# Attention on one core: scores three steps ahead, next to the product with V and the transpositions

## The chip, the cores and the metric

The kernel runs on one core of a Trainium2 chip. The metric is the device time of one launch in microseconds (us); of several runs the median is taken. Five engines work side by side, each through its own list of instructions in order, and wait for one another by semaphores: TensorE (PE in the profile; its weight loads are PEld), VectorE (DVE), ScalarE (ACT), GpSimd (POOL), and SyncE (SP), which only starts transfers between the main memory and the core's own memory SBUF. TensorE writes its results to a small memory of its own, PSUM, which VectorE and ScalarE read.

## What is computed

Two layers over 2048 positions of width 1024. The first is a gated MLP, which the change does not touch. The second is an attention in which each chunk of 64 positions sees its own chunk and the eight before it; this is the part that matters here:

```python
def one_chunk(args):
    c, qc = args
    kc = lax.dynamic_slice_in_dim(k_pad, c * CHUNK, B_BAND, axis=1)
    vc = lax.dynamic_slice_in_dim(v_pad, c * CHUNK, B_BAND, axis=1)
    sc = jnp.einsum('bqhd,bkhd->bhqk', qc, kc).astype(jnp.float32) + bias
    sc = jnp.where(valid[None, None, None, :], sc, NEG_INF)
    p = jax.nn.softmax(sc, axis=-1).astype(vc.dtype)
    return jnp.einsum('bhqk,bkhd->bqhd', p, vc)
...
return (o * jax.nn.silu(z)) @ w_out
```

There are 16 heads of 64 channels. Q, K and the gate z are projections of the normalised stream.

## The kernel before

**Tiling.** The positions are cut into four tiles `t` of 512, the heads into eight pairs `p`. For one tile and one pair there are eight steps `u`: head `u // 4` of the pair, block `u % 4` of 128 queries. The band of such a block is at most 640 keys. In tile 0 there are no keys ahead of the tile, so the four blocks have 128, 256, 384 and 512 keys; from tile 1 on all have 640.

**One step.** `score` (line 1383) multiplies Q and K (line 1398; each operand is split into a high and a low part, so two or four matmuls), into the PSUM tile `s`, of which there is one buffer. VectorE adds the bias and takes the row's extreme (line 1406, tiles `pr` and `nm`), ScalarE takes the exponential and its sum (line 1413), VectorE the reciprocal of the sum (line 1416), GpSimd scales the row (line 1417). `flip` (line 1422) transposes the row in blocks of 128 keys on TensorE (line 1433) into the PSUM tile `tp`, of which there is also one buffer; ScalarE copies it as the high part (line 1437), VectorE subtracts it for the low part (line 1438); both go to the tile `pt`, one buffer for a head. `value` (line 1443) multiplies a head's transposed rows and V (line 1458, result `pv`), once in four steps. `pr`, `nm` and `sl` have four buffers each.

**The filler.** Beside these steps TensorE has matmuls that none of them waits for at once: the projections of the *next* pair (tile `pj`; `project` makes Q first, then K, `gate` makes z; 8 pieces each), and the output product of the tile before (`bo`, split by a Strassen scheme into pieces). A piece is three matmuls of 512 columns (lines 111 to 113: high by high, high by low, low by high). A generator `ahead` yields after each piece; `take(gen, n)` draws `n` pieces. After the K projection ScalarE and VectorE write its high and low part (lines 1335 and 1336); the scores of the next pair need them.

**What sets the order.** The loop at lines 1893 to 1934 lists the work of a step. With `total` pieces in a pair (24 in tile 0 and for the first four pairs of tile 1; 30 to 38 where output pieces are added; 25 at the very last pair), the count drawn by the middle and by the end of step `u` is

```python
upto = total * (2 * u + 1) // per
...
upto = total * (2 * u + 2) // per
```

and `per` is 16, so the pieces are spread over all eight steps; at the last pair of tiles 0 to 2 it is 11. A step lists: the score of step `u + 2`, the first half of its pieces, the product with V (at `u` 4 for the pair's first head, at `u` 0 for the last head of the pair before), the transposition of step `u`, the postponed work of VectorE and ScalarE, the second half of its pieces. Scores of the next pair begin at `u` 6. A scheduler then walks through the listed work when the program is built, and moves an instruction forward where the ones listed ahead of it are not ready by its own reckoning; so the order on each engine is near the listed one and not equal to it. On the chip that order is fixed.

## Time and profile before

| | |
|---|---|
| time, median of 3 runs (lowest, highest) | 2655.66 us (2654.55, 2656.12) |
| span of the profiled execution, from its first to its last instruction | 2652.0 us |
| of it ahead of the attention's first scores | about 1560 us |
| mean granted TensorE clock over the span | 0.996 |

The profile is of one execution; it gives that execution's span and no time of its own by the clock that the runs are timed with. The median of the runs is 3.7 us above the span. A row of the profile that groups instructions names the source line, the engine, the operation, the output and the input, then the count, the busy time, the mean length of one, and the idle time of the engine just before them with what ended it. Matmuls overlap in their pipeline: a matmul of 512 columns is shown 0.39 us long, and the next begins 0.23 us after it. So the rate of TensorE is read from the starts.

### The profile page before, as it was taken

The numbers are of one execution on the slowest core, as the hardware profiler recorded it, in microseconds if no ns is written. First come the engines' busy times: TensorE is split into PE (matmuls) and PEld (weight loads), VectorE is DVE, ScalarE is ACT, GpSimd is POOL, SyncE is SP. The second block draws the span as 40 slices with busy tenths as digits, with TensorE's granted clock in tenths as the row PEclk, the third lists the DMA queues.
The fourth block names the chain that finished last, engine by engine and source line by source line (L and its number), as shares of the span: only waits on it lengthen the run. The fifth ranks groups of instructions, "written<-read, shape, count | busy, mean of one in ns | idle before, by whom it ended". The sixth has DMA issues, their size and how long they took to land. (4 is left out here: it accounts for less than half of the span.)

```text
span 2652.0 us, 37980 instructions
## 1 busy us (share of the span) xinstructions
PE 2608.0 (98%) x12960; PEld 2181.4 (82%) x12960; DVE 1885.1 (71%) x2944; ACT 1303.2 (49%) x2303; POOL 897.2 (34%) x874
## 2 busy tenths in 40 slices
PE   8999999999999999999989999999999999999997
PEld 7888888888888888888878878888888888888886
DVE  5655676865767667757767767777778777877677
ACT  5422243442533434343356456666666655666564
POOL 3611334142152322203234434344332232332245
PEclk9999999999999999999999999999999999999999
DMA  7898998989989869967776597778787666875667
GB/s 286 313 344 329 346 370 323 323 323 338 330 302 313 308 233 324 331 206 270 280 251 214 186 280 229 231 245 263 252 270 254 226 204 224 255 230 161 195 224 251
DMA packets 273856, 718.72 MB, mean 271 GB/s; under 512 B 28800, under 2 KB 68736, under 8 KB 273664
## 3 DMA queue, kind: packets, MB, share of 16 engines
q1 hardware_dynamic: 273664, 716.31, 78.4%
q8 instruction: 103, 1.69, 0.3%
q14 instruction: 89, 0.73, 0.1%
HBM read 531.12 MB, written 174.59 MB: 266 GB/s over the span
## 5 line engine op out<-in xcount | busy, mean ns | idle before, releaser
L111 PE MATMUL P<-T,S 128*128 128x512 f32 x1248 | 496.2, 398 | 2.1 <-ACT S L434 2.1
L112 PE MATMUL P<-T,S 128*128 128x512 f32 x1248 | 488.2, 391 | 1.1 <-DVE T L437 1.1
L113 PE MATMUL P<-T,S 128*128 128x512 f32 x1248 | 488.6, 391 | 0.0
L1417 POOL TENSOR_SCALAR pr<-pr,sl 128x640 f32<-128x640 f32 (+4 forms) x256 | 209.7, 819 | 530.4 <-DVE sl L1416 445.2
L111 PE MATMUL pj<-hh_b,wh_b 128*128 128x512 f32 x768 | 320.4, 417 | 0.0
L113 PE MATMUL pj<-hh_b,wl_b 128*128 128x512 f32 x768 | 305.0, 397 | 1.2 <-DVE wl_b L229 1.1
L112 PE MATMUL pj<-hl_b,wh_b 128*128 128x512 f32 x768 | 303.4, 395 | 0.1
L1413 ACT ACTIVATE pr<-pr,nm 128x640 f32<-128x640 f32 (+4 forms) x256 | 195.5, 764 | 188.1 <-DVE nm L1406 186.6
L113 PEld LDWEIGHTS P<-T,S 128*128 128x128 f32 x1248 | 234.9, 188 | 50.5
L111 PEld LDWEIGHTS P<-T,S 128*128 128x128 f32 x1248 | 235.5, 189 | 46.9 <-ACT S L434 2.3
L112 PEld LDWEIGHTS P<-T,S 128*128 128x128 f32 x1248 | 235.6, 189 | 46.1 <-DVE T L437 1.3
L1438 DVE TENSOR_TENSOR pt<-tp,pt 128x640 fp32r<-128x640 f32 (+4 forms) x256 | 188.4, 736 | 43.7 <-ACT pt L1437 41.1
L1406 DVE CUSTOM_DVE_ANT_0 pr<-s,bias 128x640 f32<-128x640 f32 (+4 forms) x256 | 187.9, 734 | 35.7 <-PE s L1398 29.8
L1437 ACT CAST pt<-tp 128x640 fp32r<-128x640 f32 (+4 forms) x256 | 159.0, 621 | 54.0 <-PE tp L1433 49.8
L1433 PE MATMUL tp<-ident,pr 128*128 128x128 f32 x1120 | 166.7, 275 | 8.6 <-DVE pt L1438 7.3
L113 PEld LDWEIGHTS pj<-hh_b,wl_b 128*128 128x128 f32 x768 | 144.7, 188 | 36.4 <-DVE wl_b L229 3.8
L1433 PEld LDWEIGHTS tp<-ident,pr 128*128 128x128 f32 x1120 | 130.7, 140 | 43.3 <-issue 13.7
L111 PEld LDWEIGHTS pj<-hh_b,wh_b 128*128 128x128 f32 x768 | 145.8, 190 | 18.1 <-ACT wh_b L228 1.6
L1458 PEld LDWEIGHTS pv<-pt,V 128*128 128x128 f32 x896 | 143.3, 189 | 20.8 <-DVE pt L1438 3.9
L112 PEld LDWEIGHTS pj<-hl_b,wh_b 128*128 128x128 f32 x768 | 145.8, 190 | 17.1 <-DVE hl_b L186 0.6
L1458 PE MATMUL pv<-pt,V 128*128 128x256 f32 (+3 forms) x896 | 154.5, 320 | 2.2 <-ACT pt L1437 1.1
L229 DVE TENSOR_TENSOR wl_b<-raw_b,wh_b 128x1024 fp32r<-128x1024 f32 x96 | 120.4, 1255 | 28.5 <-ACT wh_b L228 27.8
(294 smaller groups left out, 5725.9 us busy)
## 6 DMA issues: line engine op xcount, KB each, us to landing
S<-hsd SPq DMA_DIRECT2D x288, 512.0 KB, 5.3
rw<-in_w_a SPq DMA_DIRECT2D x108, 512.0 KB, 6.3
A<-ytd SPq DMA_DIRECT2D x72, 512.0 KB, 5.7
raw_b<-wk SPq DMA_DIRECT2D x72, 512.0 KB, 4.3
hsd<-S SPq DMA_DIRECT2D x56, 512.0 KB, 4.9
V<-vhd SPq DMA_DIRECT2D x56, 512.0 KB, 5.4
bias<-reld SPq DMA_DIRECT2D x64, 320.0 KB, 4.2
va<-vd SPq DMA_DIRECT2D x32, 512.0 KB, 5.5
```

The source lines that it names most:

```text
L111: first = mm(ps, lh, rh, start=first, stop=False)
L112: mm(ps, lh, rl, start=False, stop=False)
L113: mm(ps, ll, rh, start=False, stop=last)
L229: tv(wl[:], raw[:], wh[:].bitcast(F32), op=sub)
L1406: nc.vector.tensor_tensor_reduce(out=pr[:, c0:].rearrange("p (a b) -> p a b", a=nseg), in0=ps[:, :nseg, :w], in1=bias[:, c0:].rearrange("p ...
L1413: nc.scalar.activation(pr[:, c0:], pr[:, c0:], AF.Exp, scale=-1.0, bias=nm[:], accum_out=sl[:])
L1417: nc.gpsimd.tensor_scalar(pr[:, c0:], pr[:, c0:], sl[:], 1.0, op0=ALU.mult, op1=ALU.mult)
L1433: ins = tpose(tp[:, b, :], pr[:, b * P : (b + 1) * P], ident[:])
L1437: nc.scalar.copy(oh, tp[:, b0:5, :].rearrange("p a b -> p (a b)"))
L1438: nc.vector.tensor_tensor(pt[:, 2560 + o + b0 * P : 2560 + o + 640], tp[:, b0:5, :].rearrange("p a b -> p (a b)"), oh.bitcast(F32), op=ALU ...
L1458: mm(po[:, q0 * P : q1 * P], vtl[t, p][:, i, hs], rhs, start=(i == blocks[0] and j == 0), stop=(i == 7 and j == 1),)
```

## The change

Three things are changed in the listing of the work; nothing in what is computed, and no tile or buffer count.

1. `score` now lists the score matmuls and the line 1406 alone, and gives back a function `weigh` that lists the exponential, the reciprocal and the scaling. It is called behind `flip`.
2. The scores run three steps ahead (`AHEAD = 3`), so those of the next pair begin at `u` 5. The score, the product with V and the transposition of a step are listed one behind the other; all pieces of the step come behind them.
3. `per` is 12 where `total` is at most 24, and 9 instead of 11 at the last pair of tiles 0 to 2; where `total` is larger it stays 16. With 12 all pieces are drawn by the end of `u` 5.

```diff
             )
-            nc.scalar.activation(
-                pr[:, c0:], pr[:, c0:], AF.Exp, scale=-1.0, bias=nm[:], accum_out=sl[:]
-            )
-            nc.vector.reciprocal(sl[:], sl[:])
-            nc.gpsimd.tensor_scalar(
-                pr[:, c0:], pr[:, c0:], sl[:], 1.0, op0=ALU.mult, op1=ALU.mult
-            )
             prs[t, h, qb] = pr
+
+            def weigh():
+                nc.scalar.activation(
+                    pr[:, c0:], pr[:, c0:], AF.Exp, scale=-1.0, bias=nm[:], accum_out=sl[:]
+                )
+                nc.vector.reciprocal(sl[:], sl[:])
+                nc.gpsimd.tensor_scalar(
+                    pr[:, c0:], pr[:, c0:], sl[:], 1.0, op0=ALU.mult, op1=ALU.mult
+                )
+
+            return weigh
...
+        AHEAD = 3
...
-        for u in range(2):
+        for u in range(AHEAD):
             take(first, 4)
-            score(0, 0, u)
+            score(0, 0, u)()
...
-                total = steps_of(t, p) - (0 if t + p else 8)
-                per = 11 if p + 1 == NPAIR and t + 1 < NT else 16
+                total = steps_of(t, p) - (0 if t + p else 4 * AHEAD)
+                per = 9 if p + 1 == NPAIR and t + 1 < NT else 12 if total <= 24 else 16
...
                 for u in range(8):
-                    if u < 6:
-                        score(t, p, u + 2)
+                    weigh = None
+                    if u + AHEAD < 8:
+                        weigh = score(t, p, u + AHEAD)
                     elif p + 1 < NPAIR or t + 1 < NT:
-                        score(t + (p + 1) // NPAIR, (p + 1) % NPAIR, u - 6)
-                    upto = total * (2 * u + 1) // per
-                    take(gen, upto - done)
-                    done = max(done, upto)
+                        weigh = score(
+                            t + (p + 1) // NPAIR, (p + 1) % NPAIR, u + AHEAD - 8
+                        )
                     if u == 4:
                         value(t, p, 0)
                     elif u == 0 and before:
                         value(*before, 1)
                     flip(t, p, u)
+                    if weigh:
+                        weigh()
                     drain_all()
...
                     upto = total * (2 * u + 2) // per
                     take(gen, upto - done)
                     done = max(done, upto)
```

What this makes of the engines' lists is shown at three places. In the rows below, a tile's name has lost the number of its position tile: `s_4_1` is the score of head 4, block 1, `tp_3_2` the transposition of head 3, block 2, `pj_2_2` the projection of pair 2, kind 2 (0 is K, 1 is Q, 2 is the gate); the long number at the end is only a mark. A `x2` at the end of a row counts equal instructions.

**Place one: TensorE at the end of pair 1 of tile 1.** Before:

```order
L1398 MATMUL s_4_1_16683<-K_2_0_16618,Qh_2_0_16472 128x320 x2
L1398 MATMUL s_4_1_16683<-K_2_0_16618,Ql_2_0_16473 128x320 x2
L111 MATMUL pj_2_2_16637<-hh_b,wh_b_2_2_16632 128x512
L112 MATMUL pj_2_2_16637<-hl_b,wh_b_2_2_16632 128x512
L113 MATMUL pj_2_2_16637<-hh_b,wl_b_2_2_16633 128x512
L1433 MATMUL tp_3_3_16698<-ident,pr_3_3_16594 128x128 x5
L111 MATMUL pj_2_2_16637<-hh_b,wh_b_2_2_16632 128x512
L112 MATMUL pj_2_2_16637<-hl_b,wh_b_2_2_16632 128x512
L113 MATMUL pj_2_2_16637<-hh_b,wl_b_2_2_16633 128x512
L111 MATMUL pj_2_2_16637<-hh_b,wh_b_2_2_16632 128x512
L112 MATMUL pj_2_2_16637<-hl_b,wh_b_2_2_16632 128x512
L113 MATMUL pj_2_2_16637<-hh_b,wl_b_2_2_16633 128x512
```

The same place with the change:

```order
L1398 MATMUL s_4_1_16678<-K_2_0_16604,Qh_2_0_16488 128x320 x2
L1398 MATMUL s_4_1_16678<-K_2_0_16604,Ql_2_0_16489 128x320 x2
L1437 MATMUL tp_3_2_16687<-ident,pr_3_2_16524 128x128 x5
L1398 MATMUL s_4_2_16707<-K_2_0_16604,Qh_2_0_16488 128x320 x2
L1398 MATMUL s_4_2_16707<-K_2_0_16604,Ql_2_0_16489 128x320 x2
L1437 MATMUL tp_3_3_16716<-ident,pr_3_3_16561 128x128 x5
L1398 MATMUL s_4_3_16737<-K_2_0_16604,Qh_2_0_16488 128x320 x2
L1398 MATMUL s_4_3_16737<-K_2_0_16604,Ql_2_0_16489 128x320 x2
L1462 MATMUL pv_3_16746<-pt_3_16582,V_1_16242 128x512
L111 MATMUL pj_3_1_16789<-hh_b,wh_b_3_1_16784 128x512
L112 MATMUL pj_3_1_16789<-hl_b,wh_b_3_1_16784 128x512
L113 MATMUL pj_3_1_16789<-hh_b,wl_b_3_1_16785 128x512
```

Between a score and the next transposition there were three filler matmuls, and six between a transposition and the next score. With the change three scores and two transpositions of consecutive steps stand together without any; the filler of the step is used up. This is so at 14 places: after each of the eight pairs of tile 0, after the first four pairs of tile 1, and after the last pair of tiles 1 and 2. Elsewhere, twelve or so filler matmuls stand between a transposition and the next score, and none between a score and the transposition behind it.

**Place two: VectorE at the same place.** Before:

```order
L1406 ISA pr_4_1_16688,nm_4_1_16689<-s_4_1_16683,bias_4_16494 128x640
L1406 ISA nm_4_1_16689 128x1
L229 TENSOR_TENSOR wl_b_3_1_16739<-raw_b_3_1_16737,wh_b_3_1_16738 128x1024
L1438 TENSOR_TENSOR pt_3_16564<-tp_3_3_16698,pt_3_16564 128x640
L1416 RECIPROCAL sl_4_1_16690<-sl_4_1_16690 128x1
L1362 SCALAR_TENSOR_TENSOR Z_2_16714<-Z_2_16714,pj_2_2_16637 128x512
L1406 ISA pr_4_2_16730,nm_4_2_16731<-s_4_2_16725,bias_4_16494 128x640
```

With the change:

```order
L1406 ISA pr_4_1_16683,nm_4_1_16684<-s_4_1_16678,bias_4_16463 128x640
L1406 ISA nm_4_1_16684 128x1
L371 TENSOR_TENSOR so_4l<-wo_10_16363,so_4h 128x512
L1442 TENSOR_TENSOR pt_3_16582<-tp_3_2_16687,pt_3_16582 128x640
L1419 RECIPROCAL sl_4_1_16685<-sl_4_1_16685 128x1
L1406 ISA pr_4_2_16712,nm_4_2_16713<-s_4_2_16707,bias_4_16463 128x640
L1406 ISA nm_4_2_16713 128x1
L1442 TENSOR_TENSOR pt_3_16582<-tp_3_3_16716,pt_3_16582 128x640
L1406 ISA pr_4_3_16742,nm_4_3_16743<-s_4_3_16737,bias_4_16463 128x640
```

The work is the same in kind. A score's line 1406 now has behind it the subtraction of the transposition that is listed with it, and the reciprocal of that score comes behind this subtraction. (Lines 1437 to 1442 of the changed file are lines 1433 to 1438 of the one before.)

**Place three: TensorE where the K projection of pair 3 of tile 3 ends.** Before, the end of that projection and what follows:

```order
L111 MATMUL pj_3_0_23279<-hh_b,wh_b_3_0_23274 128x512
L112 MATMUL pj_3_0_23279<-hl_b,wh_b_3_0_23274 128x512
L113 MATMUL pj_3_0_23279<-hh_b,wl_b_3_0_23275 128x512
L1458 MATMUL pv_4_23348<-pt_4_23192,V_2_23025 128x512 x4
```

With the change:

```order
L113 MATMUL pj_3_0_23303<-hh_b,wl_b_3_0_23299 128x512
L111 MATMUL pj_3_2_23407<-hh_b,wh_b_3_2_23402 128x512
L112 MATMUL pj_3_2_23407<-hl_b,wh_b_3_2_23402 128x512
L113 MATMUL pj_3_2_23407<-hh_b,wl_b_3_2_23403 128x512
L111 MATMUL pj_3_2_23407<-hh_b,wh_b_3_2_23402 128x512
L112 MATMUL pj_3_2_23407<-hl_b,wh_b_3_2_23402 128x512
L113 MATMUL pj_3_2_23407<-hh_b,wl_b_3_2_23403 128x512
L1398 MATMUL s_6_0_23414<-K_3_0_23390,Qh_3_0_23285 128x320
L1437 MATMUL tp_5_1_23423<-ident,pr_5_1_23267 128x128 x5
L111 MATMUL pj_3_2_23407<-hh_b,wh_b_3_2_23402 128x512
```

Before, a whole product with V, two transpositions, another score and 18 filler matmuls stood between the end of the K projection and the score `s_6_0` that reads it. Now it is six filler matmuls up to that score's first matmul, which reads only keys of the tile before, then a transposition and four filler matmuls up to the other three, which read the new K.

## The prediction

> **What bounds the kernel now.** I read the page's shares first.

> ```profile
> span 2652.0 us, 37980 instructions
> PE 2608.0 (98%) x12960; PEld 2181.4 (82%) x12960; DVE 1885.1 (71%) x2944; ACT 1303.2 (49%) x2303; POOL 897.2 (34%) x874
> ```

> TensorE is shown busy nearly throughout. That share alone proves little, since overlapping matmuls fill short gaps, so I cut out the attention (the table of windows, whose columns are time, then busy time of each engine, clock, DMA share) and asked what TensorE waits for there (the view of waits: total us, times, longest).

> ```profile
> 1570.00:2600.00 1030.00, 1019.40 (x5498) 863.85 (x5496) 778.20 (x1470) 638.27 (x1184) 358.67 (x466) 1.00 0.73 233
> ```
> ```profile
> PE tp L1433 <- DVE pt L1438: 7.3, 12, 1.1
> ...
> PE s L1398 <- DVE nm L1406: 1.1, 2, 0.7
> ...
> PE pv L1458 <- ACT pt L1437: 1.1, 1, 1.1
> PE pv L1458 <- DVE pt L1438: 1.0, 3, 0.4
> ```

> Of 1030 us only 10.6 are idle, and all the waits that the order of scores, transpositions and products with V could cause come to 7.3 + 1.1 + 1.1 + 1.0 = 10.5 us over the attention. Last, a steady step in the timeline (start, length), to see whether the busy time is work:

> ```profile
> 2164.75 0.45 PE L1398 MATMUL s<-K,Qh 128*128 128x320 f32 x2
> 2165.04 0.45 PE L1398 MATMUL s<-K,Ql 128*128 128x320 f32 x2
> 2165.33 0.39 PE L111 MATMUL pj<-hh_b,wh_b 128*128 128x512 f32 x1
> 2165.56 0.39 PE L112 MATMUL pj<-hl_b,wh_b 128*128 128x512 f32 x1
> ...
> 2166.72 0.71 PE L1433 MATMUL tp<-ident,pr 128*128 128x128 f32 x5
> 2167.18 0.48 PE L111 MATMUL pj<-hh_b,wh_b 128*128 128x512 f32 x1
> ```

> Start to start, a filler matmul takes 0.23 us, a score 0.58, five transpositions 0.46, and nothing lies between. TensorE is the bound and it is full: the filler stands between score and transposition and covers what the other engines do meanwhile. So the change can win at most those 10.5 us, and every wait it makes is paid in full, since no engine's slack can give TensorE its time back.

> **What a step costs without filler.** The other engines' part of the same step, VectorE first:

> ```profile
> 2165.64 0.82 DVE L1406 CUSTOM_DVE_ANT_0 pr<-s,bias 128x640 f32<-128x640 f32 x1 [0.44 <-PE s L1398]
> 2166.39 0.08 DVE L1406 DVE_READ_ACCUMULATOR2_ANT nm<- 128x1 f32 x1
> 2167.46 0.16 DVE L1416 RECIPROCAL sl<-sl 128x1 f32<-128x1 f32 x1 [0.99 <-ACT pr L1413]
> 2168.19 0.82 DVE L1438 TENSOR_TENSOR pt<-tp,pt 128x640 fp32r<-128x640 f32 x1 [0.56 <-ACT pt L1437]
> ```
> ```profile
> 2166.51 0.83 ACT L1413 ACTIVATE pr<-pr,nm 128x640 f32<-128x640 f32 x1 [2.17 <-DVE nm L1406]
> 2167.24 0.18 ACT L1413 ACTIVATION_READ_ACCUMULATOR pr<-pr,nm 128x1 f32 x1
> 2167.46 0.70 ACT L1437 CAST pt<-tp 128x640 fp32r<-128x640 f32 x1
> ```

> From a score's start to the end of its line 1406 it is 2164.75 to 2166.47, 1.72 us; from a transposition's start to the end of its subtraction 2166.72 to 2169.01, 2.29 us. Both PSUM tiles have one buffer, so these are the least distances from one score to the next and from one transposition to the next; the waits above (tp on line 1438, s on 1406) say so too. TensorE's own work over such a distance, a score and a transposition, is 0.58 + 0.46 = 1.04 us.

> **The 14 places.** The listing puts a score, a transposition, a score, a transposition, a score (A, X, B, Y, C) and the first product with V on end, without filler, after all eight pairs of tile 0, four of tile 1, and the last of tiles 1 and 2. For 640 keys, from A's start, with the lengths above and about 0.1 us from one engine to the next:
> A 0 to 0.58; its line 1406 until 1.72; B may start at 1.8, until 2.38. X 0.58 to 1.04 (shown until 1.29), copy until 2.01, subtraction 2.04 to 2.86. Now Y may start, at 3.0, where TensorE was free at 2.38: 0.6 lost beside B's 0.76. A's exponential lasts to about 2.95, its reciprocal stands ahead of B's line 1406 on VectorE, which therefore lasts from 3.14 to 3.97. C starts at 4.05, where TensorE was free at 3.46: 0.6 lost. Y's copy ends at 4.44, C at 4.63, so the product with V starts at 4.65; its low part needs Y's subtraction (until 5.3) and three filler matmuls cover that. In 4.65 us TensorE has worked 3 × 0.58 + 2 × 0.46 = 2.66: **2.0 us lost**. Behind Y and C on TensorE wait the product with V and all filler; behind the waiting copy on ScalarE waits the exponential. Where other VectorE work stands in between (at pair 1 of tile 1 a line 371 does), the loss grows by up to its length, some 0.7 us if it is like the 512-column subtraction of K quoted below; if nothing but the transposition's own 2.29 us counted, it would be 2.4 − 1.04, about 1.3. I take 2.0 between 1.3 and 2.7, at 7 places (six, and the last pair of tile 0, whose next scores have 640 keys): 14 us.

> In tile 0 the blocks at these places have 256, 384 and 512 keys in A, B, C, and X and Y are three and four transpositions:

> ```profile
> 1706.57 0.49 PE L1433 MATMUL tp<-ident,pr 128*128 128x128 f32 x3
> 1706.81 0.48 PE L111 MATMUL pj<-hh_b,wh_b 128*128 128x512 f32 x1
> ...
> 1709.31 0.63 PE L1433 MATMUL tp<-ident,pr 128*128 128x128 f32 x4
> 1709.69 0.48 PE L111 MATMUL pj<-hh_b,wh_b 128*128 128x512 f32 x1
> ...
> 1711.16 0.34 PE L1398 MATMUL s<-K,Qh 128*128 128x384 f32 x1
> ...
> 1711.52 0.40 PE L111 MATMUL pj<-hh_b,wh_b 128*128 128x512 f32 x1
> ```
> ```profile
> L1437 ACT CAST pt<-tp 128x512 fp32r<-128x512 f32 x10 | 5.8, 577 | 0.1
> L1406 DVE CUSTOM_DVE_ANT_0 pr<-s,bias 128x384 f32<-128x384 f32 x10 | 5.5, 553 | 1.1 <-PE s L1398 1.0
> ...
> L1438 DVE TENSOR_TENSOR pt<-tp,pt 128x384 fp32r<-128x384 f32 x9 | 4.9, 548 | 1.7 <-ACT pt L1437 1.7
> ...
> L1437 ACT CAST pt<-tp 128x384 fp32r<-128x384 f32 x9 | 4.3, 481 | 0.1
> ```

> TensorE's work is 0.24 (X), 0.38 (Y), 0.36 (B); A and C are 0.23 and 0.46 at the filler's rate by columns. X starts at 0.23, is shown until 0.72, copy until 1.23, subtraction until 1.81; Y 1.95, shown until 2.58; B's line 1406 behind the subtraction until 2.4, C 2.5 to 2.96; Y's copy until 3.19, product at 3.25. Work until then 1.67: 1.6 lost, and up to a gate's VectorE work more, since the gate's last piece stands just ahead. I take 1.8, between 1.0 and 2.2, at 7 places: 12.6 us.

> **The scores of the next pair.** In tiles 2 and 3 the K projection of the next pair now ends at the start of `u` 4, and the score at `u` 5 reads it after ten filler matmuls, one score matmul and a transposition, 2.3 + 0.15 + 0.46 = 2.9 us. Between them come, on ScalarE and VectorE:

> ```profile
> L1336 DVE TENSOR_TENSOR K<-pj,K 64x512 fp32r<-64x512 f32 x60 | 41.3, 689 | 13.9 <-ACT K L1335 13.0
> ...
> L1335 ACT CAST K<-pj 64x512 fp32r<-64x512 f32 x60 | 34.8, 580 | 28.0 <-PE pj L113 19.5 <-DVE K L1336 8.0
> ...
> L229 DVE TENSOR_TENSOR wl_bo<-raw_bo,wh_bo 128x1024 fp32r<-128x1024 f32 x18 | 23.5, 1307 | 6.4 <-ACT wh_bo L228 6.3
> ```

> 0.58 + 0.69 and about 0.3 of hand-over, 1.6 us, fit. With a weight's 1.3 us on VectorE ahead of them it is 2.9, just as long. I take 0.25 us at 14 pairs, 3.5 us, between none and 1.5 each (21), where a second such job queues. The score also issues the load of the next head's bias:

> ```profile
> bias<-reld SPq DMA_DIRECT2D x64, 320.0 KB, 4.2
> ```

> It moves with the score, still three steps (some 12 us) ahead of use, and GpSimd's two small fills that wait for it hold up only scalings that now have a step more to spare. The old K and V are loaded as far ahead as before.

> **What goes.** The reciprocal no longer stands ahead of the subtraction, so VectorE does not sit (0.99 us above) waiting for the exponential before it frees `tp`. Of the 10.5 us I give back 3.5, between none and all: elsewhere a step's transpositions are as far apart as before. The exponential moved behind the copy costs nothing where filler stands: a row is now used three steps after its score instead of two, at some 4 us a step. The start (one more score ahead of the loop) and the tail I leave at nothing, between −2 and +2; the tail's waits are among the 10.5.

> **Sum.** 14 + 12.6 + 3.5 − 3.5 = 26.6 us on a span of 2652.0. The median of the runs is 2655.7, 3.7 above the span, and I keep that: 2655.7 + 26.6 = **2682**. Its own range, from the bounds of the places (16 to 34) and some 4 us for the rest, is 2668 to 2694.

> **Rivals.** *The clock.* This trace has one case in the attention where TensorE ran dry and the clock fell (idle time in brackets, then windows with the clock third from the right):

> ```profile
> 1588.92 0.50 PE L1458 MATMUL pv<-pt,V 128*128 128x512 f32 x1 [1.10 <-ACT pt L1437]
> 1589.87 1.74 PE L1458 MATMUL pv<-pt,V 128*128 128x512 f32 x7 [0.45 <-DVE pt L1438]
> ```
> ```profile
> 1588.00:1592.00 4.00, 2.63 (x10) 2.24 (x11) 3.05 (x7) 2.37 (x7) 1.09 (x3) 0.80 0.93 275
> 1592.00:1596.00 4.00, 4.00 (x16) 3.18 (x15) 2.76 (x6) 0.96 (x4) 1.84 (x1) 0.77 0.68 247
> 2580.00:2594.00 14.00, 11.46 (x58) 8.69 (x57) 14.00 (x22) 9.88 (x20) 7.08 (x6) 1.00 0.75 274
> ```

> It lost 4 × (0.20 + 0.23) = 1.7 us of full clock. In the tail four spread waits left the clock at 1.00. A place's 2.0 us are spread over 3.6, between the two. If all 14 trip it, 14 × 1.7 = 24 us more: 2706. Chance 0.10. [...]

> *K comes late.* If a second job queues ahead of K in tiles 2 and 3, 14 × 1.5 replaces the 3.5: 2699. VectorE's 71% speaks for it, the fit above against it. Chance 0.09.

> *The places are cheap.* Half of my prices, K in time, and all old waits gone: 13.3 − 10.5 = 2.8, 2658. For it speaks that the scheduler, which moves filler ahead of work it holds unready, moved none ahead of Y; against it the lengths above. Chance 0.08.

> *Faster.* The subtraction freed of the reciprocal removes the 10.5 us, and the 14 places cost less than that: at nothing, 2645. It decides at Y's start: below 0.75 us a place the kernel is faster at all, below 0.37 by more than 5.3 us. By the rows Y alone loses 0.58 + 2.29 + 0.1 − 2.38 = 0.6, so the 2.29 would have to be near 2.0, with B's line 1406 not late either. Chance 0.05.

> That the change does not do what it says is out: the lists of the built program show the places.

> **Chances.** The forecast keeps 0.68. About 0.2% (5.3 us) is what a measurement of this kernel can tell from no change. Faster has the last rival, 0.05; within it the cheap places, 0.08; slower the rest, 0.87. The range to hold 8 in 10 reaches over the forecast's own to late K and most of the clock's: 2662 to 2705.

> **What would show it.** At the 14 places: TensorE's waits of 0.5 to 0.8 us for the subtraction and for line 1406, two or three each, so the view of waits should show some 12 to 20 us on transpositions and 5 to 12 on scores; windows of tiles 0 and 1 carry the loss, tile 3 almost none. Loss in tiles 2 and 3 under waits for K would be the second rival; clock under 0.95 in tiles 0 and 1 the first. It is wrong if the span of tile 0 does not grow.

## The result, and the profile after

| | before | after |
|---|---|---|
| time, median (lowest, highest), 4 runs each, side by side | 2655.11 us (2654.27, 2656.12) | 2702.05 us (2701.30, 2702.88) |
| ratio, with its 95% interval | | 1.0176 (1.0163 to 1.0190) |
| span of the profiled execution | 2652.0 us | 2699.9 us |

The change makes the kernel 47 us slower; 27 were forecast. The page of the changed kernel begins so:

```profile
span 2699.9 us, 37933 instructions
PE 2620.6 (97%) x12960; PEld 2197.0 (81%) x12960; DVE 1895.0 (70%) x2944; ACT 1302.4 (48%) x2303; POOL 907.2 (34%) x874
```

The shares barely move, so they say nothing of the cause. The span is 47.9 us longer, and TensorE's busy time only 12.6. I cut the execution at the first line 1406 (the first reduction of a score) and at the last subtraction of each tile. Before, that is at 1539.1, 1743.9, 2033.7, 2323.7 and 2610.0 us; after, at 1546.3, 1767.4, 2075.3, 2368.8 and 2657.9. (So the attention begins earlier than the profile of the kernel before was said to show: its first score starts at 1538.1 us, not at about 1560.) The table of windows, before and then after (time, length, busy time of TensorE, its weight loads, VectorE, ScalarE and GpSimd, then the clock):

```profile
1539.10:1743.90 204.80, 201.98 (x1012) 165.21 (x1011) 145.83 (x354) 128.33 (x281) 79.02 (x121) 0.98 0.77 245
1743.90:2033.70 289.80, 287.92 (x1572) 245.32 (x1570) 226.27 (x404) 186.80 (x335) 110.39 (x133) 1.00 0.79 257
2033.70:2323.70 290.00, 288.10 (x1575) 246.23 (x1575) 219.17 (x401) 175.98 (x316) 87.97 (x120) 1.00 0.71 228
2323.70:2610.00 286.30, 279.90 (x1530) 237.59 (x1529) 216.24 (x389) 172.39 (x310) 98.71 (x119) 1.00 0.66 212
```
```profile
1546.30:1767.40 221.10, 203.27 (x1011) 166.74 (x1010) 148.40 (x355) 126.96 (x281) 79.81 (x120) 0.98 0.72 227
1767.40:2075.30 307.90, 294.88 (x1572) 254.33 (x1572) 227.97 (x404) 186.81 (x335) 111.96 (x133) 0.97 0.75 242
2075.30:2368.80 293.50, 288.47 (x1578) 248.26 (x1577) 221.74 (x402) 177.66 (x317) 92.28 (x120) 1.00 0.70 225
2368.80:2657.90 289.10, 281.03 (x1537) 240.37 (x1535) 218.88 (x389) 172.35 (x309) 100.92 (x122) 1.00 0.65 209
```

Tile 0 is 16.3 us longer, tile 1 18.1, tiles 2 and 3 3.5 and 2.8, the tail (42.0) not at all. TensorE's idle time, length less busy time, rises from 2.8, 1.9, 1.9 and 6.4 to 17.8, 13.0, 5.0 and 8.1. In tile 1 its busy time rises by 7.0 as well, at a clock of 0.97. The rest lies ahead of the attention, in code that the change does not touch: its first projection (the first weight load of a `pj` on line 111) comes at 1521.6 us before and at 1529.2 after, 7.6 later. The view of waits of the changed kernel, from 1515 us on:

```profile
PE s L1398 <- DVE nm L1406: 17.0, 17, 1.8
PE tp L1437 <- DVE sl L1419: 11.0, 13, 1.8
PE tp L1437 <- DVE pt L1442: 7.1, 13, 2.1
```

Scores waiting for the reduction before them went from 1.1 to 17.0 us. I read the second row as the same wait as the third: the reciprocal stands right behind the subtraction on VectorE, and in both rows the transposition starts 0.15 us after the end of the subtraction, whichever of the two is named.

**The 14 places.** The run of score, transposition, score, transposition, score, product (A, X, B, Y, C, V below) without filler is found 14 times in the trace, where the prediction put it. One of them in tile 0, in the timeline (start, length; TensorE, VectorE and ScalarE):

```profile
1594.47 1.05 ACT L228 CAST wh_b<-raw_b 128x1024 fp32r<-128x1024 f32 x1 [1.60 <-POOL raw_b L213]
1594.66 0.28 PE L1398 MATMUL s<-K,Qh 128*128 128x256 f32 x1
...
1595.43 0.59 ACT L1361 ACTIVATE Z<-pj 128x512 f32<-128x512 f32 x1
1595.55 1.23 DVE L229 TENSOR_TENSOR wl_b<-raw_b,wh_b 128x1024 fp32r<-128x1024 f32 x1 [2.48 <-ACT wh_b L228]
1595.91 0.47 ACT L1441 CAST pt<-tp 128x384 fp32r<-128x384 f32 x1
1596.70 0.42 DVE L1406 CUSTOM_DVE_ANT_0 pr<-s,bias 128x256 f32<-128x256 f32 x1
...
1597.04 0.68 DVE L1362 SCALAR_TENSOR_TENSOR Z<-Z,pj 128x512 f32<-128x512 f32 x1
...
1597.17 0.44 PE L1398 MATMUL s<-K,Qh 128*128 128x384 f32 x1 [1.79 <-DVE nm L1406]
...
1597.64 0.55 DVE L1442 TENSOR_TENSOR pt<-tp,pt 128x384 fp32r<-128x384 f32 x1
...
1598.33 0.63 PE L1437 MATMUL tp<-ident,pr 128*128 128x128 f32 x4 [0.54 <-DVE sl L1419]
...
1599.64 0.50 PE L1462 MATMUL pv<-pt,V 128*128 128x512 f32 x1
```

From A (1594.66) to V (1599.64) it is 4.98 us with 1.67 us of work: 3.3 lost. A's reduction (1596.70) waits on VectorE behind the split of a *weight* (line 229, 1.23 us), so B is 1.79 late; X's subtraction waits behind the gate's Z (line 1362, 0.68), so Y is 0.54 late; on ScalarE, X's copy stands behind a weight's cast (line 228, 1.05) and the gate's tanh (line 1361, 0.59). The place at the end of pair 6 of tile 0 has no weight to split:

```profile
1731.19 0.28 PE L1398 MATMUL s<-K,Qh 128*128 128x256 f32 x1
...
1732.02 0.69 DVE L1362 SCALAR_TENSOR_TENSOR Z<-Z,pj 128x512 f32<-128x512 f32 x1
1732.12 0.44 PE L1398 MATMUL s<-K,Qh 128*128 128x384 f32 x1 [0.20 <-DVE nm L1406]
...
1734.63 0.50 PE L1462 MATMUL pv<-pt,V 128*128 128x512 f32 x1
```

It takes 3.44 us and loses 1.76, which is the forecast's 1.8. In tile 1, line 371 joins in (the low part of a weight sum, which itself waits for a transfer), and the clock falls:

```profile
1828.43 0.45 PE L1398 MATMUL s<-K,Qh 128*128 128x320 f32 x2
...
1829.26 0.69 DVE L1362 SCALAR_TENSOR_TENSOR Z<-Z,pj 128x512 f32<-128x512 f32 x1 [0.59 <-ACT Z L1361]
...
1830.75 0.56 PE L1398 MATMUL s<-K,Qh 128*128 128x320 f32 x2 [1.02 <-DVE nm L1406]
...
1831.23 0.69 DVE L371 TENSOR_TENSOR so_4l<-wo,so_4h 128x512 fp32r<-128x512 f32 x1 [0.54 <-DMA ows<-so_7l]
...
1832.80 1.30 PE L1437 MATMUL tp<-ident,pr 128*128 128x128 f32 x5 [1.20 <-DVE sl L1419]
...
1834.97 0.71 PE L1462 MATMUL pv<-pt,V 128*128 128x512 f32 x1
```

All 14, each worked out from the trace in this way (start of V less start of A, less the work: scores at 0.23 us for 512 columns, transpositions at 0.46 for five):

| place | other jobs in the queues | lost, us | forecast |
|---|---|---|---|
| tile 0, first six | weight split (228, 229), gate (1361, 1362) | 4.05, 3.30, 2.95, 3.12, 2.89, 3.47 | 1.8 each |
| tile 0, seventh | gate | 1.76 | 1.8 |
| between tiles 0 and 1 | gate | 2.53 | 2.0 |
| tile 1, four | gate, weight sum (370, 371) | 3.23, 3.89, 2.88, 4.27 | 2.0 each |
| ends of tiles 1 and 2 | gate | 2.25, 2.25 | 2.0 each |
| sum | | **42.8** | 26.6 |

Of the 42.8 us, 4.7 to 5.8 are lost to half clock inside the places, an estimate (half of TensorE's busy time at half clock, or half of all time at it): three filler matmuls at half clock start 0.43 us apart (1904.04, 1904.47, 1904.90) where they otherwise start 0.23 apart. From its first projection to the end, the attention took 2652.0 − 1521.6 = 1130.4 us before and 2699.9 − 1529.2 = 1170.7 after, 40.3 more: by this account the places hold all of it, and everything outside them comes to −2.5. Half clock also goes on behind a place's end: between the first projection and the last 10 us, where both kernels have it, the clock records have seven windows of 3.4 us at half in the changed kernel and two in the one before. The five more are up to 1.7 us each, 8.5 of the 40.3.

### The profile page after: what moved, and what is told of

It is laid out like the page before. It is cut to its first block, busy times and chain, and to the rows that moved or that the text cites. A ratio compares the mean times of both kernels' runs of the same rounds, so it can differ in the third digit from the quotient of the medians.

```text
span 2699.9 us, 37933 instructions
## 1 busy us (share of the span) xinstructions
PE 2620.6 (97%) x12960; PEld 2197.0 (81%) x12960; DVE 1895.0 (70%) x2944; ACT 1302.4 (48%) x2303; POOL 907.2 (34%) x874
## 5 line engine op out<-in xcount | busy, mean ns | idle before, releaser
L111 PE MATMUL P<-T,S 128*128 128x512 f32 x1248 | 496.3, 398 | 2.1 <-ACT S L434 2.1
L112 PE MATMUL P<-T,S 128*128 128x512 f32 x1248 | 488.1, 391 | 1.1 <-DVE T L437 1.1
L113 PE MATMUL P<-T,S 128*128 128x512 f32 x1248 | 488.6, 392 | 0.0
L1420 POOL TENSOR_SCALAR pr<-pr,sl 128x640 f32<-128x640 f32 (+4 forms) x256 | 215.1, 842 | 591.1 <-DVE sl L1419 491.5
L111 PE MATMUL pj<-hh_b,wh_b 128*128 128x512 f32 x768 | 317.9, 414 | 0.3 <-ACT wh_b L228 0.3
L113 PE MATMUL pj<-hh_b,wl_b 128*128 128x512 f32 x768 | 303.0, 394 | 0.8 <-DVE wl_b L229 0.8
L112 PE MATMUL pj<-hl_b,wh_b 128*128 128x512 f32 x768 | 302.5, 394 | 0.0
L113 PEld LDWEIGHTS P<-T,S 128*128 128x128 f32 x1248 | 234.8, 188 | 50.7
L111 PEld LDWEIGHTS P<-T,S 128*128 128x128 f32 x1248 | 235.6, 189 | 46.7 <-ACT S L434 2.3
L112 PEld LDWEIGHTS P<-T,S 128*128 128x128 f32 x1248 | 235.7, 189 | 46.0 <-DVE T L437 1.3
L1416 ACT ACTIVATE pr<-pr,nm 128x640 f32<-128x640 f32 (+4 forms) x256 | 195.9, 765 | 116.9 <-DVE nm L1406 115.4
L1406 DVE CUSTOM_DVE_ANT_0 pr<-s,bias 128x640 f32<-128x640 f32 (+4 forms) x256 | 188.3, 736 | 76.9 <-PE s L1398 64.5
L1437 PE MATMUL tp<-ident,pr 128*128 128x128 f32 x1120 | 169.5, 278 | 19.3 <-DVE sl L1419 11.0
L113 PEld LDWEIGHTS pj<-hh_b,wl_b 128*128 128x128 f32 x768 | 145.0, 189 | 33.8 <-DVE wl_b L229 2.5
L112 PEld LDWEIGHTS pj<-hl_b,wh_b 128*128 128x128 f32 x768 | 146.1, 190 | 24.4
L111 PEld LDWEIGHTS pj<-hh_b,wh_b 128*128 128x128 f32 x768 | 146.2, 190 | 24.0 <-ACT wh_b L228 1.0
L1437 PEld LDWEIGHTS tp<-ident,pr 128*128 128x128 f32 x1120 | 130.5, 142 | 33.5 <-issue 28.4
L229 DVE TENSOR_TENSOR wl_b<-raw_b,wh_b 128x1024 fp32r<-128x1024 f32 x96 | 122.2, 1274 | 35.9 <-ACT wh_b L228 33.8
```

What stands on the lines that cost most here:

```text
L111: first = mm(ps, lh, rh, start=first, stop=False)
L112: mm(ps, lh, rl, start=False, stop=False)
L113: mm(ps, ll, rh, start=False, stop=last)
L229: tv(wl[:], raw[:], wh[:].bitcast(F32), op=sub)
L1406: nc.vector.tensor_tensor_reduce(out=pr[:, c0:].rearrange("p (a b) -> p a b", a=nseg), in0=ps[:, :nseg, :w], in1=bias[:, c0:].rearrange("p ...
L1416: nc.scalar.activation(pr[:, c0:], pr[:, c0:], AF.Exp, scale=-1.0, bias=nm[:], accum_out=sl[:])
```

## The experiments

Medians are upset here by a term that has nothing to do with the change. Up to the first projection of the attention the changed kernel and the one before have the same instructions on each engine, in the same order, with the same waits; yet this part took anything from 1520.6 to 1529.2 us in the 14 profiles, and 1529.2 and 1523.9 in two of the changed kernel itself. So the table gives, beside the median and its ratio to the kernel before (run on the same chip each time, 2654.96 to 2657.24 us), the time of the profiled execution from that first projection to the end, by which I judge; each such time is of one execution, and the two of the changed kernel differ by 2.3. The expectations speak of the time from the first *reduction* to the end, which is given too; it runs alike but for the two kernels in which a weight's split is moved and comes ahead of the first reduction. The last column is the sum lost in the places that are still found in the form A, X, B, Y, C, V.

| kernel | median, us | ratio (interval) | first projection to end | (more than before) | first reduction to end | lost in places (number) |
|---|---|---|---|---|---|---|
| before | 2655.11 |  | 1130.4 |  | 1112.9 | none |
| after | 2702.05 | 1.0176 (1.0163, 1.0190) | 1170.7 | +40.3 | 1153.6 | 42.8 (14) |
| after, again | 2694.95 | 1.0139 (1.0122, 1.0156) | 1168.4 | +38.0 | 1150.5 | 40.4 (14) |
| before, exponential behind | 2654.68 | 0.9999 (0.9989, 1.0009) | 1128.1 | −2.3 | 1111.1 | none |
| before, front-loaded | 2665.96 | 1.0047 (1.0032, 1.0062) | 1142.2 | +11.8 | 1124.7 | none |
| after, two ahead, old table | 2673.02 | 1.0064 (1.0048, 1.0081) | 1148.0 | +17.6 | 1129.8 | none |
| after, filler spread | 2683.79 | 1.0111 (1.0096, 1.0126) | 1159.1 | +28.7 | 1140.3 | 7.0 (3) |
| after, half step back | 2670.30 | 1.0048 (1.0033, 1.0063) | 1145.5 | +15.1 | 1127.5 | none |
| after, half step back, spread | 2669.62 | 1.0043 (1.0028, 1.0058) | 1145.8 | +15.4 | 1127.9 | none |
| after, half step at `u` 0 only | 2672.13 | 1.0064 (1.0049, 1.0079) | 1147.3 | +16.9 | 1129.4 | none |
| after, half step at `u` 1 to 7 only | 2710.74 | 1.0209 (1.0193, 1.0224) | 1185.3 | +54.9 | 1167.6 | 36.1 (9) |
| after, split earlier | 2694.74 | 1.0138 (1.0123, 1.0153) | 1167.3 | +36.9 | 1143.8 | 36.3 (14) |
| after, gate later | 2687.01 | 1.0113 (1.0096, 1.0130) | 1167.3 | +36.9 | 1149.1 | 34.2 (13) |
| after, half step, gate and split moved | 2675.84 | 1.0077 (1.0062, 1.0092) | 1150.9 | +20.5 | 1128.8 | none |

### The parts of the change alone

**Filler spread again** (three ahead and the new listing stay):

```diff
-                per = 9 if p + 1 == NPAIR and t + 1 < NT else 12 if total <= 24 else 16
+                per = 9 if p + 1 == NPAIR and t + 1 < NT else 12 if total == 24 else 16
...
-                    upto = total * (2 * u + 2) // per
+                    upto = (4, 7, 10, 14, 17, 19, 22, 24)[u] if per == 12 else total * (2 * u + 2) // per
```

> Scores stay three steps ahead and the new listing stays; only the filler of the pairs with 24 pieces is spread (4, 7, 10, 14, 17, 19, 22, 24 pieces by the end of each step, in place of all 24 by the sixth), so 11 of the 14 places without filler go; the three at the ends of tiles 0 to 2 stay. Theory A (the places cost it): 11 places at the 2 to 3 us that tiles 0 and 1 lost for each go, -22 to -33 us, so 2669 to 2680 us, tile 0 at 206 to 209 us (221.2 in the changed kernel, 204.8 before) and tile 1 at 291 to 297 (307.9, 289.8). Theory B (the listing itself costs it: score, product and transposition on end in every step): 2692 to 2702 us, both tiles as in the changed kernel. The part ahead of the attention, whose instructions are the same in all these kernels, took 1539.1 us before and 1546.3 after; if the change causes that, it is 1546 here, otherwise anything between.

Between the two theories: 9 to 12 us under the changed kernel. Eleven places that lost 33 to 36 us are gone, and only the three at the ends of the tiles are left (7.0), yet 28.7 − 7.0 = 21.7 us are now lost elsewhere.

**The kernel before with the new table** (two ahead, old listing):

```diff
-                per = 11 if p + 1 == NPAIR and t + 1 < NT else 16
+                per = 9 if p + 1 == NPAIR and t + 1 < NT else 12 if total <= 24 else 16
```

> The kernel before (two steps ahead, old listing) with nothing changed but the filler's table (9, 12 or 16 in place of 11 or 16), which draws all 24 pieces in six of eight steps. Theory A (places without filler cost it, whatever the listing): the same pairs run dry for two steps, 7 places in tile 0, 4 in tile 1 and three at tile ends at 1.5 to 3 us: +20 to +40 us, 2675 to 2695 us, the loss in tiles 0 and 1. Theory B (the listing costs it): 2650 to 2661 us.

Front-loading costs 11.8 us here, between the two theories: less than A asked and more than B. No place in the form A, X, B, Y, C, V is found in its trace: this listing draws a half step ahead of the product, and the scheduler moved such pieces in between.

**The new listing alone**:

```diff
-        AHEAD = 3
+        AHEAD = 2
...
-                per = 9 if p + 1 == NPAIR and t + 1 < NT else 12 if total <= 24 else 16
+                per = 11 if p + 1 == NPAIR and t + 1 < NT else 16
```

> The changed kernel with two steps ahead in place of three and the filler's old table (11 or 16): the new listing alone. Theory A (places): within 5 us of the kernel before, 2650 to 2661 us; waits for the subtraction may rise a little since no filler stands between score and transposition in the listing. Theory B (the listing costs it): most of the 47 us stay, 2680 to 2702 us.

Neither: 17.6 us lost without one empty place. The timeline of this kernel has one long wait in each middle pair of tile 0:

```profile
1636.30 1.05 ACT L228 CAST wh_b<-raw_b 128x1024 fp32r<-128x1024 f32 x1 [1.95 <-POOL raw_b L213]
1637.26 0.36 ACT L1441 CAST pt<-tp 128x256 fp32r<-128x256 f32 x1
1637.38 1.23 DVE L229 TENSOR_TENSOR wl_b<-raw_b,wh_b 128x1024 fp32r<-128x1024 f32 x1 [2.41 <-ACT wh_b L228]
1638.52 0.68 DVE L1406 CUSTOM_DVE_ANT_0 pr<-s,bias 128x512 f32<-128x512 f32 x1
...
1639.13 0.42 DVE L1442 TENSOR_TENSOR pt<-tp,pt 128x256 fp32r<-128x256 f32 x1
...
1639.70 0.52 PE L1437 MATMUL tp<-ident,pr 128*128 128x128 f32 x3 [1.45 <-DVE pt L1442]
```

Without a half step between score and transposition, the copy and the subtraction, and the reduction too, all come behind the same weight split, and the filler of the step does not last as long as that queue. There are six such waits of 1.4 to 1.5 us, 8.7 in all; the rest of the 17.6 was not followed.

**The exponential moved alone**, in the kernel before:

```diff
                     flip(t, p, u)
+                    if weigh:
+                        weigh()
                     drain_all()
```

> The kernel before with one part of the change alone: exponential, reciprocal and scaling listed behind the step's transposition, copy and subtraction. My own term: the waits of transpositions for the subtraction (7.3 us before) go in part, -3.5 us, 2649 to 2655 us. Rival: the exponential now starts a copy later and with two steps ahead its row is late for the transposition, so waits for the scaled row appear, 2658 to 2670 us.

No measurable difference in the median, so this part costs nothing; but my term does not show. The view of waits of this kernel, and the window of its tile 0:

```profile
PE tp L1437 <- DVE pt L1442: 7.1, 15, 1.0
PE tp L1437 <- DVE sl L1419: 1.9, 3, 1.1
```
```profile
1539.00:1740.50 201.50, 198.99 (x1012) 162.91 (x1011) 145.28 (x354) 128.27 (x281) 78.92 (x121) 1.00 0.78 250
```

The transpositions wait 7.1 + 1.9 us for the subtraction, where the kernel before had 7.3: nothing was given back. The −2.3 us lie within what half clock makes of the two traces: two windows of 3.4 us in tile 0 of the kernel before (clock 0.98, up to 3.4 us lost), none here (1.00). The profiled execution was also one of the fastest of ten (2651.87 us, of 2651.67 to 2661.30).

The rows make a ladder of single steps from before to after: exponential behind −2.3; the half step of filler between score and product no longer drawn +19.9 (1128.1 to 1148.0, the only difference of those two kernels); a third step ahead, with the front-loaded tile ends and a spread table that runs one or two pieces ahead of the old one, +11.1 (1159.1); front-loading of the other pairs +9 to 12. But the steps do not add in another order, as the next group shows.

### What the half step is worth, and where

This group began with the changed kernel once more.

> The changed kernel once more, nothing edited, as the base of this group. All theories: 2698 to 2706 us. What it tells apart is the part ahead of the attention: the kernels run so far took 1538.1 to 1546.3 us for the same instructions there. If the changed kernel's 1546.3 is its own, it is 1545 to 1547 again; if it is the run's, it may be anything from 1538 to 1547.

It came out at 2694.95 us, below the range, with its first reduction at 1541.8 us: the 1546.3 was the execution's. From the first projection on it is 1168.4 against 1170.7. The intervals of the two ratios, 1.0163 to 1.0190 and 1.0122 to 1.0156, do not meet, so medians of different rounds can differ by some 7 us without a cause in the code.

**Half a step of filler drawn again ahead of the products and transpositions**, with the front-loaded tables, and then with spread ones:

```diff
+                    upto = total * (2 * u + 1) // per
+                    take(gen, upto - done)
+                    done = max(done, upto)
                     if u == 4:
                         value(t, p, 0)
```

> The changed kernel with one edit: half of a step's filler is drawn again between the score and the products and transpositions, as before the change; three steps ahead and the front-loaded tables (9, 12, 16) stay, so the 14 places stay as they are. Theory C (two costs that add: 18 us because score and transposition stand on end everywhere, as the run of the listing alone gave, and the rest from the places): 2680 to 2688 us. Theory A (all from the places): 2698 to 2704 us. Theory D (the places cost little once score and transposition are apart in the other steps): 2660 to 2675 us.

> As the run before, and the filler of the pairs with 24 pieces spread too (2, 4, 6, 7, 9, 10, 12, 14, 16, 17, 18, 19, 21, 22, 23, 24 pieces by each half step): three steps ahead with filler nearly everywhere, only the three tile ends front-loaded. Theory C: the kernel before plus three tile ends at 2 to 3 us, 2658 to 2666 us. Rival (a third step ahead costs by itself, some 10 us, as the spread run stood above the run of the listing alone): 2665 to 2672 us. Rival (three ahead gains): under 2654 us.

The first is theory D's 2660 to 2675 and not the sum of theory C: 23 to 25 us come back from one edit. In the second, spreading then gives nothing more, and its time fits the rival, a third step ahead that costs by itself; the three tile ends, front-loaded in this kernel too, are not told apart from it.

**The half step in one place or in the others.** The two counterparts draw it only where `u == 0` or only where `u > 0`:

```diff
+                    if u == 0:
+                        upto = total * (2 * u + 1) // per
+                        take(gen, upto - done)
+                        done = max(done, upto)
```

> The changed kernel with the half step of filler between score and product drawn again in the first step of each pair alone (u = 0); the other seven steps stay as in the changed kernel. In the built program these pieces, which belong to the next pair, stand inside the 14 places (four to seven matmuls between X, B, Y and C), which are empty in the changed kernel. From the first reduction to the end, 1150.5 to 1153.6 us in the changed kernel, 1127.5 with the half drawn in every step. Theory P (the 24 us that the half step is worth are the places): 1127 to 1134 us, 2667 to 2677 in all, tiles 0 and 1 as in that run (209 and 301). Theory Q (they are lost in every step, because transposition follows score at once): 1142 to 1149 us.

> The counterpart: the half step of filler is drawn again in the steps u = 1 to 7 and not in u = 0. In the built program the places stay empty, and in the other steps filler stands between score and transposition. Theory P: 1144 to 1151 us from the first reduction to the end. Theory Q: 1130 to 1138 us.

The first of the pair is theory P's 1127 to 1134 (1129.4); the second lies above both ranges (1167.6). Drawn at `u` 0 alone, the half step gives back 21 to 23 us, nearly all that it gives when drawn everywhere (1147.3 against 1145.5). Up to 12 of them are the clock's: the changed kernel's two traces have seven windows of 3.4 us at half clock each, this one has none until its last 10 us. The place in tile 0 of that kernel shows the rest:

```profile
1610.48 0.28 PE L1398 MATMUL s<-K,Qh 128*128 128x256 f32 x1
...
1610.58 1.23 DVE L229 TENSOR_TENSOR wl_b<-raw_b,wh_b 128x1024 fp32r<-128x1024 f32 x1 [1.69 <-ACT wh_b L228]
...
1610.96 0.48 PE L111 MATMUL pj<-hh_b,wh_b 128*128 128x512 f32 x1
...
1612.07 0.68 DVE L1362 SCALAR_TENSOR_TENSOR Z<-Z,pj 128x512 f32<-128x512 f32 x1
...
1612.20 0.44 PE L1398 MATMUL s<-K,Qh 128*128 128x384 f32 x1 [0.53 <-DVE nm L1406]
...
1612.90 0.39 PE L111 MATMUL pj<-hh_b,wh_b 128*128 128x512 f32 x1
...
1613.59 0.60 PE L1437 MATMUL tp<-ident,pr 128*128 128x128 f32 x4
```

The same weight split and the same Z stand on VectorE, but now the next pair's filler (lines 111 to 113) stands between X, B and Y: the scheduler moved forward what was listed there, and B waits 0.53 instead of the 1.4 to 1.8 at the middle places of tile 0, Y not at all. Drawn in the other seven steps, the half step made the kernel 15 to 17 us slower than the changed one, which neither theory had. Tiles 0 and 1 of that kernel:

```profile
1541.30:1773.70 232.40, 211.44 (x1011) 172.31 (x1010) 143.41 (x355) 127.38 (x282) 78.85 (x120) 0.94 0.68 216
1773.70:2087.10 313.40, 300.28 (x1573) 256.08 (x1572) 227.32 (x405) 186.97 (x335) 112.48 (x133) 0.96 0.73 238
```

The places stay empty, and with clocks of 0.94 and 0.96 some 0.06 × 232 = 14 and 0.04 × 313 = 13 us in these tiles are the clock's: its records have eight stretches of 6.8 us at half, up to 27 us lost. The seven windows of the changed kernel are up to 12, and the difference of 15 us is about the whole excess. Why each of these stretches is twice as long was not found.

### What stands in the queues

**The weight split one half-block earlier** (tile 0 only):

```diff
-            paced_by_pj(scaled(raw, (bg if c else kg)[:, :, :]), 3)
+            paced_by_pj(scaled(raw, (bg if c else kg)[:, :, :]), 4)
```

> The changed kernel with one number changed: in tile 0 the scaling of a weight, and with it its split (1.05 us on ScalarE, 1.23 us on VectorE), is tied to the projection four half-blocks back instead of three, so the split that stands on VectorE ahead of A's reduction and on ScalarE ahead of X's copy at each place of tile 0 moves one step forward, where filler follows. Theory V (a place is dear because such jobs stand in the two queues): the waits of scores for the reduction in tile 0 (9.8 us, up to 1.8 each) fall to about 0.5 each, tile 0 from 221 to 210 to 215 us, in all -6 to -11 us. Theory S (a place is dear because of the single score buffer and the transposition's own 2.29 us, whatever else is queued): no change, within 3 us.

By the median and from the first projection on (1167.3 against 1168.4 and 1170.7) this is theory S: hardly a change. (From the first reduction on it looks like theory V, but here that reduction itself comes some 6 us later, behind a split.) In the places theory V holds. Five places of tile 0 have no split in them any more, and lose 1.75, 1.76, 1.76, 1.76 and 1.75 us, as the seventh did before. One of them, from A to V:

```profile
1622.91 0.28 PE L1398 MATMUL s<-K,Qh 128*128 128x256 f32 x1
...
1626.35 0.50 PE L1462 MATMUL pv<-pt,V 128*128 128x512 f32 x1
```

So a split is worth 1.1 to 1.7 us at such a place, 6.9 over the five (up to 1.05 of it half clock, at the last), and 1.76 is what is left with the gate; that the single buffers set it follows from the lengths, no run had a second buffer for `s` or `tp`. But most of the 6.9 is paid again elsewhere: the first place of tile 0 now loses 5.0, and all outside the places, −2.4 in the changed kernel's second profile, is 36.9 − 36.3 = +0.6.

**The gate's Z behind the place** (tiles 0 and 1; the two operations are listed after the first step of the next pair):

```diff
+            if t < 2:
+                late.append(lambda: on_beat(finish()))
+            else:
+                finish()
...
         def drain_all():
+            while late:
+                late.pop(0)()
```

> The changed kernel with one job moved: in tiles 0 and 1 the gate's two operations on Z (tanh on ScalarE, line 1361, 0.59 us; sum and product on VectorE, line 1362, 0.68 us) are listed after the first step of the next pair instead of at the place, so they stand behind B's reduction instead of ahead of X's subtraction (tile 0) or A's reduction (tile 1). Since the part ahead of the attention takes 1538 to 1548 us in runs of the same instructions, the theories are judged by the time from the first reduction of a score to the end, 1150.5 and 1153.6 us in two profiles of the changed kernel. Theory V (a place is dear because of other jobs in the queues of VectorE and ScalarE): 7 places of tile 0 and 5 of tile 1 at 0.3 to 0.7 us each, 1143 to 1149 us. Theory S (single buffers alone): 1150 to 1154 us.

At the edge of both: 1149.1, and 1 to 3 us by the first projection. Without the gate in the way, a place fell to 1.60 twice in tile 0 (1.76 with Z) and to 2.0 to 2.15 at three of the first five with 640 keys, which are the forecast's own figures without a gate (1.6 and 2.0). At two of these three lines 370 and 371 still stand, so they cost hardly anything where they come early; at the other two of tile 1 they come late, Y waits 1.68 and 2.78, and 3.8 and 4.9 are lost, up to 1.2 and 1.3 of it to half clock. Four places of tile 0 with a weight split lose 2.4 to 3.3. The mechanism shows in single places; what it is worth in total this trace may understate. It is of the slowest of the kernel's four runs (2692.28 us; the others 2684.04 to 2689.27), with the lowest clock (0.991, the others 0.993 to 0.996), and by the median the kernel is 8 us below the changed one's second round, which is still hardly more than the 7 by which that one's two rounds differ.

**All of it together**: half step, gate and split.

> Three steps ahead and front-loaded tables, with the half step drawn in every step, the gate's Z moved behind the place and the weights' scaling and split of tile 0 one half-block earlier: what is left of the change's loss if the jobs in the queues are moved too. Theory V: tile 0 from 209.4 (half step alone) to 202 to 206 us and tile 1 from 301 to 296 to 300, 1118 to 1124 us from the first reduction to the end, 2658 to 2667 in all. Theory S: 1126 to 1129 us. Faster than the kernel before (1112.9) on neither.

Theory V fails here: 1128.8, nothing gained over the half step alone (1127.5), and 5 us lost from the first projection on, as by the medians (2675.84 against 2670.30). Here moving the jobs moved the waits and removed none of the loss. No version with three steps ahead came nearer than 15.1 us to the kernel before (12 by the medians), and none beats it; the exponential moved alone equals it.

## Why the forecast was right in direction and short in size

The measured 2702 lies in the stated range (2662 to 2705), but beyond the sum's own bounds (2668 to 2694), and that it lies in the range is in part luck. The upper end was put there for a late K, of which 0.9 us came, and for the clock, which took up to 8.5 of the 24 us named for it. What filled it is jobs queued at the places, and 7.6 us of a part that the change does not touch; the sum left both out.

- **TensorE as the bound, waits paid in full:** right. Idle time in tiles 0 to 3 rises by 30.9 us, and the places hold 42.8 us against the 40.3 by which the attention grew.
- **14 places:** right, in number and position. The half step at `u` 0, which puts filler into them, gives back 21 to 23 us by itself, up to 12 of them through the clock.
- **Their price, 2.0 and 1.8 us:** this is the step that failed, in size and not in kind. The prediction's own lengths hold where only the gate is queued (1.76 and 2.25), and without the gate (1.60, and 2.0 to 2.15). But it took that price for all 14 places. It had said that other VectorE work in between would add up to its length, at pair 1 of tile 1 and for the gate; it did not look in the order of VectorE and ScalarE for what does stand there. At ten of 14 places another job is there: a weight's cast and split (1.05 and 1.23 us) in tile 0, lines 370 and 371 in tile 1. In tile 0 this is no accident of the place: the split is tied to the projection's pieces, which front-loading draws just ahead of it, and tied one half-block earlier it left five places. Lines 370 and 371 are tied to the transpositions, whatever the filler, and cost where they come late, behind a transfer. Ten places at 3.4 us in the mean (34.05 in all) where 1.8 or 2.0 stood (18.8) are 15.3 of the 16.2 us by which the places were short; 4.7 to 5.8 of them are the clock's.
- **The clock (a rival at 0.10):** partly true. Half clock takes up to 5.8 us inside the places in one profile of the changed kernel and 3.6 in the other; five places of 14 are touched each time, not all. With what runs on behind them it is five windows more than before in both profiles, up to 1.7 us each as the prediction priced one, 8.5 in all. The sign named for it, a clock under 0.95 in tiles 0 and 1, did not show (0.98 and 0.97).
- **K in time (0.25 us at 14 pairs, 3.5):** one wait of 0.9 us for K in the whole trace. The rival of a late K is out.
- **Old waits given back, 3.5:** not seen. Outside the places transpositions wait 8.2 us for the subtraction, 7.3 before, and with the exponential moved alone 9.0. K's term and this one together were forecast at nothing, and all outside the places is 40.3 − 42.8 = −2.5 us in one profile and 38.0 − 40.4 = −2.4 in the other; that these come near is not the mechanism's doing, and what makes the −2.5 is open.
- **Signs:** waits on transpositions 11.0 + 7.1 = 18.1 us, in the range named, but only 9.9 of them stand in the places, and the 12 to 20 were meant for these; on scores 17.0, above the 5 to 12 named, which is where the weight splits show. Tile 3 was to lose almost nothing: 2.8.
- **The part ahead of the attention, at nothing:** the change leaves it alone, but its 7.6 us in this profile are in the difference of the medians; in the second round of runs, where they were 2.3, the kernel was 38 us slower than the one before and not 47.

**What stays open.** Why the untouched part differs by up to 8.6 us between executions of the same instructions was not found. And outside the places the costs do not add: the changed kernel loses nothing there (−2.5), but spread filler loses 21.7 there, and three steps ahead with filler in all the places still lose 15.1 to 16.9. In a place followed there (spread half step), a transposition waited 0.82 us for a subtraction queued behind a weight's split. A step of four pieces has 12 matmuls at 0.23, some 2.8 us, to cover such a queue, and one of three pieces 2.1; that would explain it, but it was argued and not tested, and moving the split and the gate in that setting gained nothing.

## What to carry to other kernels

When filler is drawn early to make something ready sooner, price the stretch that is left empty by everything queued there on the engines that TensorE waits for, the filler's own follow-up work first: the last pieces drawn left their casts and splits (1.05 and 1.23 us) in just that stretch at six places here. Read those queues from the order of the built program, since the clean price of such a stretch can be right to 0.25 us (1.76 and 2.25 here, for 1.8 and 2.0) and the real one still more than twice as long (4.05 for 1.8). And half a step of filler listed where the engine runs dry was worth nearly as much here as the same half step in all eight.

## What the runs showed of the hardware

In the changed kernel the clock halved without TensorE being idle for long (1.02 and 1.20 us at the longest in the place at 1828.43, where half clock begins at 1832.3). Stretches of 3.4 us of its trace (columns as above; the clock third from the right):

```profile
1593.40:1596.80 3.40, 1.99 (x12) 1.51 (x10) 1.25 (x2) 1.91 (x3) 1.39 (x2) 1.00 0.94 376
1596.80:1600.20 3.40, 2.35 (x10) 1.50 (x11) 2.58 (x10) 1.79 (x5) 0.48 (x1) 1.00 0.36 84
1595.00:1598.40 3.40, 1.07 (x7) 0.54 (x6) 2.85 (x7) 1.99 (x5) 0.00 (x0) 1.00 0.58 235
1828.90:1832.30 3.40, 1.68 (x11) 1.17 (x10) 2.50 (x5) 2.36 (x5) 0.77 (x1) 1.00 0.84 176
1832.30:1835.70 3.40, 2.90 (x11) 2.72 (x12) 1.99 (x6) 1.56 (x4) 0.80 (x1) 0.51 1.03 391
```
